# The first expert pair's weight chunks through both buffer rings, and less fill per expert step

## The chip, the cores and the metric

The kernel runs on one core of one Trainium2 chip, in one launch. The metric is the device time of that launch in microseconds (us); the median over several runs counts. TensorE is called PE below, VectorE DVE, ScalarE ACT, GpSimd POOL, SyncE SP.

## What is computed

Two transformer blocks follow each other on 512 tokens of width 1024, with a context of 256 tokens beside them. The first block mixes the tokens with three attention branches and then runs an expert-choice feed-forward layer: 16 experts, each of which takes the 64 tokens that its router column ranks highest.

```
def expert_choice_ffn(h, w_router, w_gate, w_up, w_down):
    ...
    gate, idx = lax.top_k(jnp.swapaxes(aff, 1, 2), cap)
    ...
    xe = h[bidx, idx]
    hid = jax.nn.silu(jnp.einsum('becd,edf->becf', xe, w_gate)) * jnp.einsum('becd,edf->becf', xe, w_up)
    ye = jnp.einsum('becf,efd->becd', hid, w_down) * gate[..., None].astype(h.dtype)
    return jnp.zeros_like(h).at[bidx, idx].add(ye)
```

The second block has two layers, each over the tokens and over the context (latent attention, pooling, gated linear attention, a gated merge). All is float32.

## The kernel before, in words

The program is written as Python generators that yield a nominal cost after each piece of work. `weave(main, fill, ratio)` takes a piece of `main` and then pieces of `fill` worth `ratio` times its cost, so two stages share the engines. A scheduler then orders each engine's instructions; every engine and every DMA queue works in that order.

The stage in question is the feed-forward layer of the first block. `ffn_start` norms the tokens, runs the router and the top-k. `experts` works on the 16 experts in 8 pairs, `p` = 0 to 7. A pair is 12 calls of `group`: 4 for the gate product, 4 for the up product, 4 for the down product. A group loads four chunks of expert weights (`we`, 128x1024 float32, 512 KB each, the DMA issues of L1296 on SP) and runs eight matmuls on them (L1307). So there are 96 groups and 384 chunks. Two experts share the PE array, 64 rows each.

Chunks land in one of two rings of buffers. `early` (tag "early", `NEARLY` = 20 buffers) lives only while the pool `tpR` is open. `big` (tag "wbig", `nbig` = 8 buffers) lives until the experts end. `s.pre` starts at `NPRE` = 44. In `body` (L2163 to L2180) the pool `tpR` is open while `ffn_start` and then the first 11 groups (44 chunks) are written out; after that the space of `tpR` is given to `tpB`, where the fill's tiles lie. A chunk may only be loaded into a buffer when the matmuls that read the buffer's last chunk are done, and SP issues in order: while one chunk waits for its buffer, all loads behind it wait.

From the twelfth group on the experts are woven with the fill, `ctx2(0)`, at `RATIO_E`. `ctx2(0)` is the first layer of the second block for the context: some seventy projections. A projection loads 512 KB of weights (`wr`, L412), ACT and DVE split them into a high and a low part (`wh` L395, `wl` L391), and PE runs 24 matmuls on them (L404 to L406, 128x256). Its last piece, `finish`, has 8 projections with `w_out` (`wr<-in_wout` on SP, stationary `wh`/`wl`, moving `mh`), a norm and a store.

After the experts, `ffn_end` adds their outputs to the tokens: for each of 8 column blocks a transpose of the summed outputs (L1417), a placing of the last pair's outputs (L1419), two DVE additions (L1421) and a square for the norm (L515, L516). It is woven with what is left of the fill at `RATIO_G` = 2, and its first yield is worth 10. Then the tokens' second block begins with the matmuls on `hx`.

Of the kernel before, what the change touches and what calls it, by code (L numbers as in the profile page):

```python
# [307 lines left out]
def weave(main, fill, ratio):  # L308

    while True:  # L310
        try:
            c = next(main)
        except StopIteration as e:
            return e.value
        fill.step(c * ratio)


class Kern:
# [967 lines left out]
    def experts(s):  # L1286
# [1 line left out]
        wx = s.d["wexp"]  # L1288

        def chunk(p, i, h):  # L1290
            if s.pre:
                s.pre -= 1
                w = s.early.tile([128, 1024], F32, name=s.uid("we"), tag="early", bufs=NEARLY)
            else:
                w = s.big.tile([128, 1024], F32, name=s.uid("we"), tag="wbig", bufs=s.nbig)
            nc.sync.dma_start(w, wx[p, i][:, h * 1024:h * 1024 + 1024])  # L1296
            return w

        def group(p, c0, stat, ps, kh):

            ws = [[chunk(p, c0 + e, h) for e in (1, 0)][::-1] for h in (1, 0)][::-1]
            with s.tc.high_priority(URGE):
                for h in range(2):
                    for kk in range(2):
                        k = 4 * kh + 2 * h + kk
                        for e in range(2):
                            nc.tensor.matmul(ps[64 * e:64 * e + 64, :], stat[:, k, 64 * e:64 * e + 64],  # L1307
                                             ws[h][e][:, kk * 512:kk * 512 + 512], start=k == 0, stop=k == 7)
# [801 lines left out]
def tags(w=512, **k):  # L2110
    return {a: b if isinstance(b, (tuple, str)) else (b, w) for a, b in k.items()}
# [3 lines left out]
NEARLY = 20  # L2115
URGE = 600
NPRE = 44
# [21 lines left out]
TAGS_M = tags(kc=(4, 256), P=(4, 768), PT=4)  # L2139
TAGS_F = tags(fx=8, ft=3)  # L2140
RATIO_G = 2
RATIO_E = 0.8
TAGS_G = tags(gh=8, gl=4)


def body(tc, d, out):
    from contextlib import ExitStack
    with ExitStack() as ctx:
# [26 lines left out]
        with k.pool("tpB") as tp:  # L2175
            k.where = (tp, TAGS_C)
            k.wq = tc.nc.sync
            fill.add(k.ctx2(0, M[0], cd, C[0]))
            weave(ex, fill, RATIO_E)
            big.close()  # L2180
# [36 lines left out]
```

## Time and profile before

| what | value |
|---|---|
| median of 3 runs | 2788.2 us (2779.96 to 2794.11) |
| the profiled execution | 2794.44 us, span of its instructions 2792.6 us |
| PE busy | 2625.3 us (94% of the span) |
| DVE, ACT busy | 1569.8 us, 1230.6 us |
| HBM traffic over the span | 191 GB/s on average |
| first and last start of an expert matmul (L1307) | 833.9 us, 1535.8 us |

The profile gives busy times of each engine over the span and in slices, groups of instructions with their idle time and its releaser, waits, and busy times with DMA rates in chosen stretches. Times within the execution count from the span's start.

### The profile page before, as it was taken

The numbers are of one execution on the slowest core, as the hardware profiler recorded it, in microseconds if no ns is written. First come the engines' busy times: TensorE is split into PE (matmuls) and PEld (weight loads), VectorE is DVE, ScalarE is ACT, GpSimd is POOL, SyncE is SP. The second block draws the span as 40 slices with busy tenths as digits, with TensorE's granted clock in tenths as the row PEclk, the third lists the DMA queues.
The fourth block names the chain that finished last, engine by engine and source line by source line (L and its number), as shares of the span: only waits on it lengthen the run. The fifth ranks groups of instructions, "written<-read, shape, count | busy, mean of one in ns | idle before, by whom it ended". The sixth has DMA issues, their size and how long they took to land. (4 is left out here: it accounts for less than half of the span.)

```text
span 2792.6 us, 41759 instructions
## 1 busy us (share of the span) xinstructions
PE 2625.3 (94%) x16372; PEld 1859.9 (67%) x16372; DVE 1569.8 (56%) x2957; ACT 1230.6 (44%) x2159; POOL 161.0 (6%) x260
## 2 busy tenths in 40 slices
PE   6999999999958999999998899999999999999997
PEld 2666677887633566555654577777777777777776
DVE  3564677676441324456232656656866546766974
ACT  3333355444222224365222444545655645555652
POOL 1000001110001000000000000000010000000001
PEclk9899999999979999999999899999999999999998
DMA  8545424634879999988999332213354332114353
GB/s 287 177 164 191 146 85 161 209 120 156 298 283 325 340 380 356 335 297 300 352 366 372 126 106 83 77 51 136 118 186 135 128 123 84 62 39 140 117 177 114
DMA packets 167974, 537.68 MB, mean 193 GB/s; under 512 B 21272, under 2 KB 22376, under 8 KB 167776
## 3 DMA queue, kind: packets, MB, share of 16 engines
q1 hardware_dynamic: 138528, 460.40, 47.2%
q0 software_dynamic: 17152, 52.57, 5.8%
q10 hardware_dynamic: 12096, 22.03, 2.1%
q8 instruction: 129, 2.11, 0.3%
q14 instruction: 69, 0.57, 0.1%
HBM read 484.06 MB, written 48.76 MB: 191 GB/s over the span
## 5 line engine op out<-in xcount | busy, mean ns | idle before, releaser
L391 DVE TENSOR_TENSOR wl<-wr,wh 128x1024 fp32r<-128x1024 f32 x320 | 390.8, 1223 | 386.8 <-ACT wh L395 357.3
L395 ACT CAST wh<-wr 128x1024 fp32r<-128x1024 f32 x320 | 334.4, 1047 | 458.2 <-PE ps L405 348.6
L404 PE MATMUL ps<-hx,wh 128*128 128x512 f32 x1168 | 473.8, 406 | 5.8 <-ACT hx L569 5.1
L405 PE MATMUL ps<-hx,wh 128*128 128x512 f32 x1168 | 468.8, 402 | 0.1
L406 PE MATMUL ps<-hx,wl 128*128 128x512 f32 x1168 | 466.9, 400 | 0.0
L404 PEld LDWEIGHTS ps<-hx,wh 128*128 128x128 f32 x1168 | 221.8, 190 | 66.9 <-issue 13.2
L1307 PE MATMUL ps<-we,xe 128*64 128x512 f32 x1024 | 241.1, 615 | 18.1 <-DMA we<-in_wexp 18.0
L405 PEld LDWEIGHTS ps<-hx,wh 128*128 128x128 f32 x1168 | 221.6, 190 | 52.3 <-issue 8.4
L406 PEld LDWEIGHTS ps<-hx,wl 128*128 128x128 f32 x1168 | 221.7, 190 | 50.2 <-issue 3.3
L673 ACT ACTIVATE P<-ps,st 128x768 f32<-128x768 f32 (+3 forms) x144 | 111.1, 771 | 142.6 <-DVE st L669 107.7
L1307 PEld LDWEIGHTS ps<-we,xe 128*64 128x64 f32 x1024 | 76.0, 141 | 144.8 <-issue 118.4
L404 PE MATMUL ps<-hc,wh 128*128 128x256 f32 x496 | 144.1, 291 | 0.1
L406 PE MATMUL ps<-hc,wl 128*128 128x256 f32 x496 | 139.8, 282 | 0.5 <-DVE wl L391 0.5
L405 PE MATMUL ps<-hc,wh 128*128 128x256 f32 x496 | 140.3, 283 | 0.0
L667 DVE TENSOR_REDUCE st<-ps 128x1 f32<-128x768 f32 (+3 forms) x144 | 114.2, 793 | 38.1 <-PE ps L406 35.3
L1307 PE MATMUL ps<-we,hT 128*64 128x512 f32 x512 | 122.8, 626 | 10.4 <-DMA we<-in_wexp 8.2
L695 PE MATMUL ps<-c_ident,P 128*128 128x128 f32 x688 | 110.0, 278 | 5.3 <-ACT PT L698 3.5
L404 PEld LDWEIGHTS ps<-hc,wh 128*128 128x128 f32 x496 | 94.1, 190 | 19.5 <-issue 14.2
L695 PEld LDWEIGHTS ps<-c_ident,P 128*128 128x128 f32 x688 | 79.9, 140 | 39.8 <-ACT PT L698 13.4
L471 PE MATMUL ps<-wm,sc_cc 128*32 128x512 f32 x384 | 89.4, 647 | 15.9 <-DMA wm<-in_wmod 14.1
L698 ACT COPY PT<-ps 128x512 f32<-128x512 f32 x123 | 70.1, 586 | 72.6 <-PE ps L695 71.9
L405 PEld LDWEIGHTS ps<-hc,wh 128*128 128x128 f32 x496 | 94.0, 190 | 4.0 <-issue 3.5
(517 smaller groups left out, 5036.1 us busy)
## 6 DMA issues: line engine op xcount, KB each, us to landing
we<-in_wexp SPq DMA_DIRECT2D x384, 512.0 KB
wr<-in_win SPq DMA_DIRECT2D x240, 512.0 KB
wm<-in_wmod SPq DMA_DIRECT2D x48, 512.0 KB
wr<-in_wbr SPq DMA_DIRECT2D x48, 512.0 KB
dram<-th ACTq DMA_DIRECT2D x72, 256.0 KB
mth<-dram SPq DMA_DIRECT2D x72, 256.0 KB
wr<-in_wout SPq DMA_DIRECT2D x32, 512.0 KB
dram<-mth POOLq DMA_DIRECT2D x48, 256.0 KB, 3.1
```

What stands on the lines that cost most here:

```text
L391: s.nc.vector.tensor_tensor(out, a, b, ALU.subtract)
L395: i = s.nc.scalar.copy(hi, src)
L404: t.matmul(out, a[0], b[0], start=start, stop=False)
L405: t.matmul(out, a[0], b[1], start=False, stop=False)
L406: t.matmul(out, a[1], b[0], start=False, stop=stop)
L471: nc.tensor.matmul(ps[32 * j:32 * j + 32, :], sc[:, k, :], w[:, j % 2 * 512:j % 2 * 512 + 512], start=k == 0, stop=k == 7)
L667: nc.vector.tensor_reduce(st[:, 0:1], sc[:, :n], AX.X, ALU.max)
L673: nc.scalar.activation(p[:, :n], sc[:, :n], AF.Exp, bias=st[:, 1:2], scale=scale, accum_out=st[:, 2:3])
L695: nc.tensor.transpose(tp[:, j:j + 128], blocks[(i + j) // 128], s.const("ident"))
L698: nc.scalar.copy(parts[i // 512][:, :m], tp[:, :m])
L1307: nc.tensor.matmul(ps[64 * e:64 * e + 64, :], stat[:, k, 64 * e:64 * e + 64], ws[h][e][:, kk * 512:kk * 512 + 512], start=k == 0, stop=k == 7)
```

## The change

Two things change. The choice of the ring now counts chunks modulo 28 (`NEARLY + s.nbig`): chunk numbers 0 to 7 go to `big`, 8 to 27 to `early`, 28 to 35 to `big` again, 36 to 42 to `early`, and number 43 and all later ones to `big`. Before, 0 to 43 went to `early` and all later ones to `big`. And `RATIO_E` goes from 0.8 to 0.7.

```diff
         def chunk(p, i, h):
-            if s.pre:
-                s.pre -= 1
+            n = (NPRE - s.pre) % (NEARLY + s.nbig)
+            s.pre = max(s.pre - 1, 0)
+            if s.pre and n >= s.nbig:
                 w = s.early.tile([128, 1024], F32, name=s.uid("we"), tag="early", bufs=NEARLY)
             else:
                 w = s.big.tile([128, 1024], F32, name=s.uid("we"), tag="wbig", bufs=s.nbig)
...
-RATIO_E = 0.8
+RATIO_E = 0.7
```

What this moves on SP, at the end of the first prefetch: the rows name the chunk's tile (`we` and its number in the order of the program: 1291 is the first, 1313 the twenty-first, 1346 to 1349 are the twelfth group, 1362 and 1363 belong to the second pair) and the semaphores that the issue waits for (`PE` among them: the buffer must have been read by its matmuls; `DMAHW`: an earlier transfer must have landed). Before:

```order
L1296 DMA we1311_6985<-in_wexp 128x1024 [waits DMAHW5_49]
L1296 DMA we1312_6987<-in_wexp 128x1024 [waits DMAHW6_49]
L1296 DMA we1346_7130<-in_wexp 128x1024 [waits DMAHW7_49]
L1296 DMA we1347_7132<-in_wexp 128x1024 [waits DMAHW0_49]
L1296 DMA we1348_7134<-in_wexp 128x1024 [waits DMAHW1_49]
L1296 DMA we1349_7136<-in_wexp 128x1024 [waits DMAHW2_49]
L1296 DMA we1362_7173<-in_wexp 128x1024 [waits DMAHW3_49]
L1296 DMA we1363_7175<-in_wexp 128x1024 [waits DMAHW4_49]
L1296 DMA we1313_6997<-in_wexp 128x1024 [waits DMAHW5_49,PE_49]
L1296 DMA we1314_6999<-in_wexp 128x1024 [waits DMAHW6_49,PE_49]
```

Now, from the same place on SP:

```order
L1297 DMA we1312_6987<-in_wexp 128x1024 [waits DMAHW6_49,DVE_49]
L1297 DMA we1313_6997<-in_wexp 128x1024 [waits DMAHW7_49]
L1297 DMA we1314_6999<-in_wexp 128x1024 [waits DMAHW0_49,PE_49]
L1297 DMA we1315_7001<-in_wexp 128x1024 [waits DMAHW1_49]
L1297 DMA we1316_7003<-in_wexp 128x1024 [waits DMAHW2_49]
L1297 DMA we1318_7014<-in_wexp 128x1024 [waits DMAHW3_49]
L1297 DMA we1319_7016<-in_wexp 128x1024 [waits DMAHW4_49]
L1297 DMA we1320_7018<-in_wexp 128x1024 [waits DMAHW5_49]
L1297 DMA we1321_7020<-in_wexp 128x1024 [waits DMAHW6_49]
L1297 DMA we1322_7030<-in_wexp 128x1024 [waits DMAHW7_49,PE_49]
```

Before, the twenty chunks of the small ring were followed by six chunks of later groups, and only then by the twenty-first chunk. Now 28 chunks follow each other in the order in which PE reads them; we1322 is the twenty-ninth, the first that waits for an expert matmul.

On PE, around the last expert group (we and hT are the operands of an expert matmul, oh and ye those of the placing, fo that of the transposes, hc and mh those of the fill). Before:

```order
L1307 MATMUL ps_12837<-we_12871,hT_12258 64x512
L1307 MATMUL ps_12837<-we_12869,hT_12258 64x512
L1417 MATMUL ps_12962<-c_ident,fo_12775 128x128
L1417 MATMUL ps_12962<-c_ident,fo_12777 128x128
L1417 MATMUL ps_12962<-c_ident,fo_12779 128x128
L1417 MATMUL ps_12962<-c_ident,fo_12781 128x128
L516 MATMUL ps_12938<-sq_12959,sqw 2x512
L1419 MATMUL ps_12963<-oh_12773,ye_12783 128x512
```

Now the last expert matmul is followed by a projection on `hc` (24 matmuls, of which the first three stand here), and at once after it by the 192 matmuls on `mh` of the 8 projections with `w_out`:

```order
L1308 MATMUL ps_12459<-we_12491,hT_11898 64x512
L1308 MATMUL ps_12459<-we_12489,hT_11898 64x512
L404 MATMUL ps_12511<-hc_7291,wh_12507 128x256
L405 MATMUL ps_12511<-hc_7292,wh_12507 128x256
L406 MATMUL ps_12511<-hc_7291,wl_12508 128x256
```

and those end, before the placing begins, with

```order
L404 MATMUL ps_12852<-mh_12591,wh_12848 128x256
L405 MATMUL ps_12852<-mh_12592,wh_12848 128x256
L406 MATMUL ps_12852<-mh_12591,wl_12849 128x256
L1420 MATMUL ps_12889<-oh_12317,ye_12327 128x512
L1420 MATMUL ps_12889<-oh_12317,yl_12457 128x512
L1420 MATMUL ps_12910<-oh_12317,ye_12327 128x512
```

So 216 matmuls, nine projections, that stood among the experts' groups now stand between the experts and `ffn_end`. From the end of `ffn_end` on, the order of every engine is the same as before.

## Rows read from the trace of the kernel before

**Rows 1.** The page, parts 1 and 2: busy times, and 40 slices of the span.

```profile
PE 2625.3 (94%) x16372; PEld 1859.9 (67%) x16372; DVE 1569.8 (56%) x2957; ACT 1230.6 (44%) x2159; POOL 161.0 (6%) x260
...
PE   6999999999958999999998899999999999999997
...
DMA  8545424634879999988999332213354332114353
```

**Rows 2.** Stretches: us, PE, PEld, DVE, ACT, POOL busy (instructions), PE clock, DMA share, GB/s.

```profile
834.00:919.20 85.20, 68.77 (x295) 25.33 (x295) 14.60 (x34) 14.75 (x29) 12.69 (x16) 0.91 0.87 312
919.20:1536.40 617.20, 584.76 (x3974) 352.70 (x3972) 247.06 (x532) 226.87 (x443) 34.02 (x37) 0.98 0.95 345
1536.40:1564.60 28.20, 18.81 (x65) 7.33 (x65) 17.79 (x28) 11.03 (x18) 0.00 (x0) 0.83 0.34 121
```

**Rows 3.** SP's timeline in three windows: start, length, issue, count.

```profile
785.34 36.39 SPq L1296 DMA_DIRECT2D we<-in_wexp  x26
...
836.39 29.19 SPq L1296 DMA_DIRECT2D we<-in_wexp  x26
...
883.13 5.99 SPq L1296 DMA_DIRECT2D we<-in_wexp  x8
```

**Rows 4.** Stretches of the first pair, columns as in the stretches above.

```profile
836.00:840.00 4.00, 4.00 (x20) 1.31 (x18) 0.00 (x0) 0.00 (x0) 0.00 (x0) 1.00 0.60 184
844.00:872.00 28.00, 27.38 (x134) 11.66 (x130) 3.33 (x5) 2.25 (x4) 3.72 (x6) 1.00 1.02 396
876.00:880.00 4.00, 3.89 (x12) 1.21 (x14) 0.00 (x0) 0.00 (x0) 0.00 (x0) 0.57 0.11 42
880.00:884.00 4.00, 4.00 (x22) 1.34 (x20) 0.70 (x2) 0.00 (x0) 1.59 (x3) 1.00 0.22 59
```

**Rows 5.** PE's timeline, first pair: start, length, work, count, idle before and its releaser.

```profile
833.86 28.31 PE L1307 MATMUL ps<-we,xe 128*64 128x512 f32 x128
...
864.89 7.09 PE L1307 MATMUL ps<-we,hT 128*64 128x512 f32 x32 [0.24 <-ACT hT L1348]
876.11 8.71 PE L1307 MATMUL ps<-we,hT 128*64 128x512 f32 x32 [4.14 <-DMA we<-in_wexp]
...
895.82 5.66 PE L1307 MATMUL ps<-we,xe 128*64 128x512 f32 x16 [4.94 <-DMA we<-in_wexp]
```

**Rows 6.** PE's timeline later: two expert groups, between them one projection.

```profile
922.29 3.65 PE L1307 MATMUL ps<-we,xe 128*64 128x512 f32 x16
925.87 0.38 PE L404 MATMUL ps<-hc,wh 128*128 128x256 f32 x1
...
928.77 3.65 PE L1307 MATMUL ps<-we,xe 128*64 128x512 f32 x16
```

**Rows 7.** Four stretches, 919.2 to 1536.4 us, columns as above.

```profile
919.20:1200.00 280.80, 273.98 (x1664) 166.65 (x1662) 106.05 (x219) 97.49 (x183) 16.60 (x17) 1.00 0.97 354
1200.00:1330.00 130.00, 117.28 (x1162) 71.41 (x1159) 79.60 (x219) 77.41 (x179) 5.20 (x4) 0.95 0.86 297
1330.00:1455.00 125.00, 122.10 (x761) 76.18 (x758) 37.82 (x54) 32.44 (x49) 5.73 (x4) 1.00 0.97 356
1455.00:1536.40 81.40, 71.41 (x394) 38.45 (x394) 23.60 (x41) 19.52 (x34) 6.50 (x12) 0.96 1.01 373
```

**Rows 8.** PE's waits: us in total, times, longest; 919.2 to 1536.4 us.

```profile
PE ps L1307 <- DMA we<-in_wexp: 12.0, 11, 3.5
...
PE ps L404 <- ACT mth L628: 1.4, 3, 0.5
```

**Rows 9.** PE's waits, 1455 to 1536.4 us.

```profile
PE ps L1307 <- DMA we<-in_wexp: 8.3, 5, 3.5
```

**Rows 10.** PE's timeline after the last expert matmul.

```profile
1540.02 0.66 PE L1417 MATMUL ps<-c_ident,fo 128*128 128x128 f32 x4 [3.64 <-DVE x L1421]
...
1564.58 1.65 PE L404 MATMUL ps<-hx,wh 128*128 128x512 f32 x3 [1.36 <-ACT hx L569]
```

**Rows 11.** DVE's groups of the fill's end, 1500 to 1537 us: count, busy us, mean ns, idle.

```profile
L2002 DVE SCALAR_TENSOR_TENSOR o<-o,G,rb 128x256 f32<-128x256 f32 x8 | 3.5, 480 | 5.4 <-ACT rb L557 5.4
L2003 DVE TENSOR_TENSOR o<-o,xr 128x256 f32<-128x256 f32 x8 | 3.0, 418 | 0.0
```

## The prediction

> **What bounds the kernel now.** The page comes first. PE is busy for 94% of the span, and its digits are 9 nearly everywhere; the DMA digits are 8 or 9 only in a block that is the expert stage [rows 1]. There two resources are close to full together, so the question is what each lacks in that stage. I cut it into three by the stretches view [rows 2]. From 834.0 us (first expert matmul) to 919.2 us there is no fill; PE has 68.8 of 85.2 us, and the DMA engines are 0.87 busy. From 919.2 us to the last expert matmul at 1536.4 us the fill stands among the groups: PE 584.8 of 617.2 us, so 32.4 us idle, and 345 GB/s, which is 213 MB. From there to the first matmul on hx at 1564.6 us `ffn_end` runs alone: 28.2 us, PE 18.8 us.
>
> In the first stretch the cause of the idle time can be read from SP. It issued 26 chunks by 821.7 us and then nothing until 836.4 us; again 26 until 865.6 us, and nothing until 883.1 us [rows 3]. The second hole shows in the DMA rates: 396 GB/s from 844 to 872 us, then 42 and 59 GB/s from 876 to 884 us [rows 4]. SP stood at the 53rd chunk, whose buffer in the ring of 8 held the first chunk of the twelfth group. That group could not be read earlier, since the eleventh waited 4.14 us for its own chunks and then ran 8.71 us for two groups where 7.09 us is usual [rows 5]; the clock in that stretch was 0.57 [rows 4].
>
> In the second stretch PE waited only 12.0 us for expert chunks [rows 8], and 8.3 us of it in the last 81 us [rows 9].
>
> **The ring.** By the order, 28 chunks come before the first expert wait, in the order in which PE reads them. At 396 GB/s a chunk (0.524 MB) takes 1.32 us [rows 4]. The first 26 were issued by 821.7 us, so two more fit in the 14.7 us of SP's hole and are there when PE starts. From then on chunk 28 and the following wait for the same matmuls as the 27th issue did. SP gets to the eleventh group's chunks eight places earlier in its order, so they have landed before 872.0 us, when PE finishes the tenth group (864.89 + 7.09). The 4.14 us wait goes, and so do the 1.62 us that groups eleven and twelve lost at the lower clock: **-5.8 us**. This is carried on only if SP's next stop moves too. It does: after number 50, chunk 51 now waits for number 43, which the eleventh group reads, and chunk 52 for number 44, the twelfth group's first. Both groups come 5.8 us earlier, so the transfers resume about then, and PE's next wait, the 4.94 us at 895.8 us [rows 5], stands 5.8 us earlier. It does not vanish: from the second pair on there are still 8 buffers. Bounds: 0, if other transfers fill the time, and -10.7, if the 4.94 us went as well.
>
> **The fill, until the last expert matmul.** Nine projections move behind it. A projection among the groups costs PE 2.9 us (925.87 to 928.77) [rows 6], but behind one another 24 matmuls of 0.117 us follow closer; I take 2.8 us, so 25.2 us of PE work leave the stretch. They take 4.7 MB of loads along, which leaves 208.3 MB. If the idle time stayed as it is, the stretch would take 592 us. But lighter fill between groups calls for chunks at a higher rate. The stretch from 1200 to 1330 us (gated linear attention: small steps, PE 117.3 of 130 us, 297 GB/s, 38.6 MB) [rows 7] has room and stays as it is. The rest, 487.2 us before, moved 174.4 MB at 358 GB/s; now it has 169.7 MB for 462 us, 367 GB/s. The waits for chunks by rate: 3.7 us in 405.8 us (0.9%) where 354 to 356 GB/s flowed, 8.3 us in 81.4 us (10%) at 373 [rows 7 to 9]. On a line between them, 361 GB/s is where the waits (4%, 18 us instead of 12) and the rate agree: 469 us. So the stretch takes 599 us by that line. I take 597 us, a little below, since the row at 373 GB/s holds three groups that had no fill at all: **-20 us**. Bounds: -37 us if no wait for chunks is left (25.2 + 12.0), and -10 us if 355 GB/s is all that these mixed transfers reach (169.7 MB in 478 us, and 130).
>
> One page speaks against the change here. The Trainium skill (DMA: Bandwidth & Descriptors, section Bandwidth) says that for transfers from HBM to SBUF the HBM side binds, at about 358 GB/s for a core, though it lists 425 GB/s measured with one core. By the 358 this stretch would be at its limit already, the term -13 us, and the sum +7 us. The 396 GB/s above [rows 4] don't agree with it.
>
> **Behind the last expert matmul.** The 25.2 us of projections come back, at full price: nothing else is on PE then, and the transfers are idle enough to feed them (0.34 busy before [rows 2]). The projections on mh need the last merge's result through ACT and DVE; waits of that kind were at most 0.5 us [rows 8], while PE's longest on DVE here was 3.64 us [rows 10]: I take **+2 us**. `ffn_end` loses those 3.64 us, since the last experts' outputs are long ready when it starts. But the norm and the additions of the fill's end (16 DVE instructions, 6.5 us [rows 11]), until now beside the experts, stand beside its 16 additions; DVE was busy 17.8 of 28.2 us [rows 2], so most fits in its gaps: +2 us, between 0 and 6.5. Together **+25.6 us**, between 22.1 and 31.7.
>
> **Sum.** -5.8 - 20 + 25.6 = -0.2 us on the profiled execution's 2794.4 us. That one is 6.2 us above the median of the runs, 2788.2 us, so I predict **2788 us**. A measurement of this kernel can tell about 0.5%, 14 us, from no change. The order after `ffn_end` is the same, and the work before 785 us too, so nothing else should move.
>
> **Rivals.** *The transfers follow* (0.20). If they give what the first pair shows, 396 GB/s, the waits for chunks go and the fill covers the experts to the end: -5.8 - 37 + 22 to 25 = -18 to -21 us, 2767 to 2770 us; half of that gain and a ring term near -10.7 reach 2774 too. For it: 8.3 of the 12.0 us fell where the fill had run out. Against: 373 GB/s with a DMA share of 1.01 there. *The transfers are the limit* (0.13), which ends slower: at 355 GB/s the experts shorten by 10 us only, while 25.2 us of PE work now run after them with the DMA engines half empty: -5.8 - 10 + 25.6 to 31.7 = +10 to +16 us, 2798 to 2804 us. It decides once the stretch shortens by less than 20 us. For it: DMA shares of 0.97 in the long stretches [rows 7]. *The ring does nothing* (0.17): 26 chunks were there before, 28 now, and the 4.14 us come back as a longer wait when the second pair begins, since its first chunks no longer lie ready. Then the sum is +5.6 us, 2794 us.
>
> **How the numbers follow.** The forecast itself (0.50) reaches 9 us to both sides for the bounds of its terms, 2779 to 2797 us. Ends of 2770 and 2803 us leave out the far part of both outer rivals, some 0.2 in all. Below 2774 us lies most of the first rival and a little of the forecast: faster 0.20. Above 2802 us lie the far half of the second rival and a bad tail term: slower 0.12. The rest, 0.68, is no change that can be told.
>
> **What would show it.** Ring: SP's first run of issues has 28 chunks, the 4.14 us wait before the eleventh group is gone, and the 42 to 59 GB/s hole lies earlier; the matmuls of the second pair then begin some 6 us sooner. Fill: no stretch without projections before the last expert matmul, that matmul at about 1510 us (833.9 + 79.4 + 597), PE's waits for chunks 12 to 20 us in total. End: hx begins at about 1564 us. If hx begins before 1550 us or after 1578 us, the prediction is wrong; the stretch with the fill, at 580 or at 607 us, would tell which rival it was.

## The result, and the profile after

The changed kernel takes 2805.11 us (median of 9 runs, 2795.02 to 2815.78) against 2788.2 us before (2779.96 to 2798.21): a ratio of 1.0056, 95% interval 1.0035 to 1.0077. It is slower, by a little more than the half per cent that a measurement can tell, and 2 us above the upper end of the range. The profiled execution took 2806.96 us, with a span of 2805.2 us.

The line numbers behind the ring's changed lines are one higher than before: chunks are issued at L1297, expert matmuls are L1308. Lengths below are counted from the first expert matmul, since its own start lies between 826.7 and 833.9 us in the profiled executions of all kernels, also of the one with the old ring (826.7), whose work before it is the same as in the kernel before.

| part of the profiled execution | before | after | difference | forecast |
|---|---|---|---|---|
| first expert matmul to the end of the 17th group | 85.4 us | 82.0 us | -3.4 | -5.8 |
| from there to the last expert matmul | 617.1 us | 599.0 us | -18.2 | -20 |
| from there to the first matmul on `hx` | 28.2 us | 66.0 us | +37.8 | +25.6 |
| sum | 730.7 us | 747.0 us | +16.2 | -0.2 |
| from `hx` to the end | 1228.0 us | 1227.8 us | -0.2 | 0 |

The page's first parts look like [rows 1]: 8 us more of PE, and digits that hardly differ.

```profile
PE 2633.7 (94%) x16372; PEld 1866.4 (67%) x16372; DVE 1569.0 (56%) x2957; ACT 1232.5 (44%) x2159; POOL 160.1 (6%) x260
...
PE   6999999999958999999998899999999999999997
```

The same three parts as stretches (columns as in [rows 2]):

```profile
830.40:912.40 82.00, 70.00 (x296) 27.00 (x295) 14.59 (x34) 14.56 (x29) 11.25 (x16) 0.91 0.94 331
912.40:1511.30 598.90, 560.95 (x3743) 328.65 (x3743) 225.63 (x491) 210.92 (x408) 32.36 (x33) 0.97 0.95 344
1511.30:1577.40 66.10, 51.10 (x297) 37.53 (x295) 38.13 (x69) 29.01 (x53) 2.15 (x4) 0.89 0.43 148
```

PE's busy time in the middle row fell by 23.8 us, the work of the nine projections, but its idle time rose from 32.4 to 38.0 us. In the last row 32.3 us of PE work came back, beside 15.0 us of idle time instead of 9.4 us. (This row's edges are rounded outward; the table counts from the matmuls themselves.) The two idle times and the price of the work behind the experts are what has to be explained.

**The ring.** SP's timeline of the changed kernel, in three windows (start, length, issue, count; answers to [rows 3]):

```profile
782.85 40.76 SPq L1297 DMA_DIRECT2D we<-in_wexp  x28
...
833.24 13.75 SPq L1297 DMA_DIRECT2D we<-in_wexp  x15
...
857.27 19.24 SPq L1297 DMA_DIRECT2D we<-in_wexp  x13
```

28 chunks are issued ahead, then 15, and SP stops at 847.0 us with 43 chunks out: number 43 is next. PE's timeline of the changed kernel in the first pair and the second (answers to [rows 5]):

```profile
830.41 28.60 PE L1308 MATMUL ps<-we,xe 128*64 128x512 f32 x128
...
861.73 14.00 PE L1308 MATMUL ps<-we,hT 128*64 128x512 f32 x64 [0.24 <-ACT hT L1349]
878.63 5.35 PE L1308 MATMUL ps<-we,xe 128*64 128x512 f32 x16 [2.90 <-DMA we<-in_wexp]
...
887.84 6.51 PE L1308 MATMUL ps<-we,xe 128*64 128x512 f32 x16 [2.28 <-DMA we<-in_wexp]
896.60 8.78 PE L1308 MATMUL ps<-we,xe 128*64 128x512 f32 x32 [2.25 <-DMA we<-in_wexp]
908.72 3.65 PE L1308 MATMUL ps<-we,xe 128*64 128x512 f32 x16 [3.33 <-DMA we<-in_wexp]
```

The wait of 4.14 us before the eleventh group is gone; the last four groups of the first pair are one row of 64 matmuls in 14.00 us. Up to the end of the twelfth group the changed kernel is 5.6 us ahead (45.3 us against 51.0). Then four waits for chunks, 10.8 us together, stand before groups 13, 14, 15 and 17, and at the end of the 17th group 3.4 us are left.

The kernel before has four waits there as well, of nearly the same length. PE's waits from the end of the 12th group to the end of the 17th (us in total, times, longest), and the same stretches (columns as in [rows 2]), first before, then changed:

```profile
PE ps L1307 <- DMA we<-in_wexp: 10.1, 4, 4.9
PE ps L1308 <- DMA we<-in_wexp: 10.8, 4, 3.3
...
884.80:919.30 34.50, 22.81 (x89) 7.19 (x84) 10.12 (x26) 9.63 (x19) 7.37 (x7) 0.85 0.98 328
875.70:912.40 36.70, 25.30 (x88) 8.35 (x87) 10.12 (x26) 9.52 (x19) 5.49 (x7) 0.81 0.95 325
```

The five groups and the few matmuls beside them take 25.3 us of PE instead of 22.8, at a granted clock of 0.81 instead of 0.85. That is the larger part of the 2.2 us that are lost again; the waits for chunks add 0.7 us, and the short waits on the fill's norm take 1.0 us off.

**The middle.** PE's waits from 912.4 to 1511.3 us (us in total, times, longest; answers to [rows 8]):

```profile
PE ps L1308 <- DMA we<-in_wexp: 11.3, 12, 2.4
PE ps L1418 <- DMA fo<-dram: 3.7, 1, 3.7
```

The waits for chunks do not grow. A wait of 3.7 us for `fo`, the experts' outputs read back for `ffn_end`, now falls ahead of the last expert matmul.

The same stretch in three parts: to the first matmul of the fill's gated linear attention, that attention to its last matmul, and the rest (columns as in [rows 2]). First the outer two before, whose middle one stands at e7 below, then all three of the changed kernel:

```profile
919.20:1205.60 286.40, 278.66 (x1696) 170.43 (x1694) 108.66 (x222) 102.67 (x190) 17.02 (x18) 1.00 0.97 353
1310.50:1536.40 225.90, 212.10 (x1290) 129.94 (x1290) 70.42 (x111) 61.52 (x99) 13.23 (x17) 0.98 0.98 359
...
912.40:1214.70 302.30, 290.03 (x1714) 170.27 (x1714) 107.09 (x221) 99.77 (x184) 17.63 (x18) 0.99 0.98 356
1214.70:1337.30 122.60, 108.06 (x1068) 59.99 (x1067) 70.79 (x203) 70.74 (x165) 6.11 (x4) 0.93 0.86 299
1337.30:1511.30 174.00, 162.86 (x963) 98.39 (x963) 47.76 (x68) 40.41 (x59) 8.62 (x11) 0.97 0.96 355
```

Outside the gated linear attention the transfers run no faster than before: 356 and 355 GB/s, where they had 353 and 359. Beside it stand 15 expert groups now, where there were 13.

**Behind the last expert matmul.** SP's timeline of the changed kernel, 1480 to 1580 us:

```profile
1499.59 0.63 SPq L412 DMA_DIRECT2D wr<-in_wout  x1
1504.45 10.07 SPq L1406 DMA_DIRECT2D x<-dram  x8
1514.62 23.94 SPq L412 DMA_DIRECT2D wr<-in_wout  x7
```

Of SP's waits in the changed kernel from 1490 to 1560 us, the one that holds them (us in total, times, longest):

```profile
SPq L1406 <- PE ps L1308: 10.6, 2, 6.5
```

Eight loads of `x` (L1406, for `ffn_end`) stand on SP between the first `w_out` load and the other seven. They go to the pool "fe", which takes the place of `big`, and so wait for the last expert matmuls to have read their chunks: 10.6 us. The seven loads behind them, on which the projections on `mh` rest, start at 1514.62 us, after the last expert matmul, when PE already wants them. PE's timeline of the changed kernel shows the price in one row:

```profile
1522.11 0.58 PE L404 MATMUL ps<-mh,wh 128*128 128x256 f32 x1 [3.55 <-ACT wh L395]
```

Two stretches of the changed kernel, the one behind that wait, and `ffn_end` (columns as in [rows 2]):

```profile
1522.00:1528.50 6.50, 5.93 (x26) 5.64 (x27) 2.45 (x2) 1.14 (x3) 0.00 (x0) 0.50 0.46 160
...
1547.50:1577.40 29.90, 20.65 (x78) 8.65 (x76) 21.29 (x43) 11.68 (x21) 0.00 (x0) 0.87 0.26 89
```

After the 3.55 us wait the granted clock is 0.50 for 6.5 us, the lower level of 1.2 GHz: 26 instructions take 5.93 us. The nine projections end at 1547.2 us, 35.8 us after the last expert matmul. What is left, 30.2 us, is `ffn_end`; it was 28.2 us before, with 17.8 us of DVE (28 instructions), and has 21.3 us of DVE (43 instructions) now.

### The profile page after: what moved, and what is told of

Its sections match the earlier page's. It is cut to its first block, busy times and chain, and to the rows that moved or that the text cites. A ratio compares the mean times of both kernels' runs of the same rounds, so it can differ in the third digit from the quotient of the medians.

```text
span 2805.2 us, 41737 instructions
## 1 busy us (share of the span) xinstructions
PE 2633.7 (94%) x16372; PEld 1866.4 (67%) x16372; DVE 1569.0 (56%) x2957; ACT 1232.5 (44%) x2159; POOL 160.1 (6%) x260
## 5 line engine op out<-in xcount | busy, mean ns | idle before, releaser
L1308 PE MATMUL ps<-we,xe 128*64 128x512 f32 x1024 | 243.4, 622 | 21.4 <-DMA we<-in_wexp 21.3
L1308 PEld LDWEIGHTS ps<-we,xe 128*64 128x64 f32 x1024 | 75.2, 142 | 152.0 <-issue 127.5
L1308 PE MATMUL ps<-we,hT 128*64 128x512 f32 x512 | 118.5, 608 | 2.9 <-ACT hT L1349 1.9
L404 PEld LDWEIGHTS ps<-hc,wh 128*128 128x128 f32 x496 | 95.1, 192 | 28.1 <-issue 23.9
L404 PE MATMUL ps<-mh,wh 128*128 128x512 f32 (+1 forms) x256 | 95.9, 375 | 3.6 <-ACT wh L395 3.6
```

The source lines that it names most:

```text
L404: t.matmul(out, a[0], b[0], start=start, stop=False)
```

## The experiments

Ratios are to the kernel before on the same chip. The lengths are those of the table above, from each kernel's profiled execution. Several ratios (e1, e5, e6, e9) differ from 1 by less than the half per cent that the prediction held to be measurable, though their intervals leave out 1; e1 and e9 overlap each other.

| kernel | to the end of group 17 | to the last expert matmul | from there to `hx` | sum | ratio (95% interval) |
|---|---|---|---|---|---|
| before | 85.4 | 617.1 | 28.2 | 730.7 | 1 |
| changed | 82.0 | 599.0 | 66.0 | 747.0 | 1.0056 (1.0035 to 1.0077) |
| e1, ring alone | 84.0 | 617.8 | 28.2 | 730.0 | 0.9981 (0.9967 to 0.9995) |
| e2, ratio alone | 84.6 | 607.0 | 64.6 | 756.2 | 1.0076 (1.0050 to 1.0103) |
| e3, loads of `x` later | 84.3 | 596.0 | 61.2 | 741.5 | 1.0049 (1.0033 to 1.0064) |
| e4, fill spread in `ffn_end` | 81.6 | 595.3 | 61.6 | 738.5 | 1.0063 (1.0041 to 1.0085) |
| e5, e3 and e4 together | 81.9 | 598.9 | 59.0 | 739.9 | 1.0022 (1.0004 to 1.0040) |
| e6, fill not woven | 82.2 | 599.9 | 58.0 | 740.1 | 1.0026 (1.0008 to 1.0045) |
| e7, `RATIO_E` 0.77 | 82.3 | 638.3 | 33.2 | 753.8 | 1.0050 (1.0033 to 1.0067) |
| e8, `RATIO_E` 0.9 | 82.9 | 676.5 | 27.0 | 786.4 | 1.0172 (1.0145 to 1.0200) |
| e9, ring alone, 48 chunks | 88.7 | 607.1 | 28.2 | 724.1 | 0.9966 (0.9951 to 0.9980) |
| e10, ring alone, 56 chunks | 83.3 | 641.5 | 32.7 | 757.6 | 1.0070 (1.0045 to 1.0094) |

### e1 and e2: each half of the change alone

e1 is the changed kernel with the old ratio, e2 the kernel before with the new one.

```diff
e1: -RATIO_E = 0.7
    +RATIO_E = 0.8
e2: -RATIO_E = 0.8
    +RATIO_E = 0.7
```

> The new choice of rings with RATIO_E back at 0.8. Theory A (the ring gains a little, the lighter fill loses more): first expert matmul to the end of group 17 takes 82 us as in the changed kernel (85.2 before), everything behind it is as before (617 us to the last expert matmul, 28 us from there to hx), so 3 us less than the kernel before in all, ratio 0.999. Rival B (the ring itself costs, because from chunk 43 on only 8 buffers are left while SP already stands): the stretch to the last expert matmul grows by 5 us or more, ratio 1.002 or above.

> The kernel before with RATIO_E 0.7 and nothing else. Theory A: 85 us to the end of group 17, about 599 us from there to the last expert matmul (18 less than before), 66 us from there to hx (38 more), so about 20 us more than before in all, ratio 1.007. Rival B: the ring is what costs, so this one stays within 5 us of the kernel before, ratio below 1.002.

e1 takes 2782.8 us and is a little faster than the kernel before, e2 is slower. The product of the two ratios, 0.9981 x 1.0076 = 1.0057, is the ratio of the change, 1.0056: within their intervals the two halves add up, and all of the loss is the ratio's. The profiled executions do not add up so well: -0.7 and +25.5 us against +16.2. Most of that is the stretch to the last expert matmul, 607.0 us in e2, with 17.6 us of waits for chunks, and 595.3 to 599.9 us in the five kernels that have the same ratio and the new ring. So the ring may help there too, which one execution of e2 can't show. In e1's profile 4.5 us are gained up to the end of the twelfth group (46.5 us against 51.0) and 1.4 us are left at the end of the 17th; the other parts keep their lengths within 1 us. Its sum explains 0.7 us of the 5 us that the runs show; the rest can't be placed with one execution of each.

### e3: the loads of `x` behind the projections' loads

```diff
         x, f = [], s.f
+        yield 10.0
         for k in range(8):
             t = s.T(nm="x", tag="fx")
             nc.sync.dma_start(t, xd[k])
             x.append(t)
-        yield 10.0
```

> The changed kernel, with the 8 loads of x for the end of the layer written behind its first yield, so that they no longer stand ahead of the w_out loads on SP. Theory A (SP's queue starves the projections: seven of the eight w_out loads stand behind loads that wait for the last expert matmul): the nine projections after the last expert matmul take 27 to 29 us instead of 35.8, the 3.55 us wait on the split weights and the half clock after it go, 7 us less than the changed kernel in all. Rival C (two raw buffers and the split on ACT and DVE set the pace, whatever the order): still 34 us or more.

SP's timeline of e3, 1480 to 1580 us:

```profile
1496.08 0.56 SPq L412 DMA_DIRECT2D wr<-in_wout  x1
1501.03 0.33 SPq L1407 DMA_DIRECT2D x<-dram  x1
1506.06 1.59 SPq L412 DMA_DIRECT2D wr<-in_wout  x2
```

The two stretches of e3 behind the last expert matmul, the nine projections and then `ffn_end` (columns as in [rows 2]):

```profile
1507.90:1537.10 29.20, 27.02 (x218) 25.86 (x218) 16.49 (x26) 16.66 (x32) 2.15 (x4) 1.00 0.73 240
1537.10:1569.10 32.00, 21.43 (x78) 9.31 (x76) 21.48 (x43) 12.12 (x21) 0.00 (x0) 0.80 0.24 83
```

One `x` load instead of eight stands ahead of the next `w_out` loads, the wait for `wh` is gone, the granted clock is 1.00 throughout, and the nine projections take 29.1 us instead of 35.8. So 6.7 us of the overrun were the queue. e2, which has the same order on SP as the changed kernel, bears it out: 34.6 us for the nine projections. `ffn_end` gives 2 us of it back (32.0 us), and the ratio moves only from 1.0056 to 1.0049, within both intervals, so these times do not settle it. The times of e5 and e4 below, which differ by this edit alone, support it: 1.0022 and 1.0063, each against the kernel before on its own chip, with intervals that do not overlap. They differ by some 11 us, though, where the two profiled executions differ by 2.6 us behind the experts.

### e4, e5, e6: another order behind the experts

```diff
e4: -RATIO_G = 2
    +RATIO_G = 1
e5: e3 and e4 together
e6: -RATIO_G = 2
    +RATIO_G = 0
```

> The changed kernel with RATIO_G 1 instead of 2: half of the w_out projections stand ahead of the end of the layer, the rest among its eight steps. Theory A (the end of the layer leaves PE idle for want of work, which the projections could fill): from the last expert matmul to hx 52 to 56 us instead of 66, 10 to 14 us less than the changed kernel. Rival D (DVE is what paces those steps): 63 us or more.

> The changed kernel with both earlier edits: the loads of x behind the first yield of the layer's end, and RATIO_G 1. Theory A (two separate losses behind the last expert matmul: w_out loads stuck on SP, and too little for PE among the layer's last steps): 54 to 58 us from the last expert matmul to hx, against 66 in the changed kernel and 61 to 62 with either edit alone; ratio to the kernel before 1.002 to 1.004. Rival E (one loss, that both edits mend): 60 us or more, ratio 1.005 or above.

> The changed kernel with RATIO_G 0: nothing of the fill is written ahead of the layer's end, the eight w_out projections follow it and cover its last steps and the norm behind it. Theory A (what costs is where the left-over projections stand, ahead of a chain of small steps that PE then has to itself): from the last expert matmul to hx 48 to 54 us, ratio 1.000 to 1.003. Rival D (DVE paces it, wherever they stand): 60 us or more, ratio 1.005 or above.

With a lower `RATIO_G` the projections are spread among `ffn_end`'s pieces, so that DVE's additions and PE's projections can lie beside each other. From the last expert matmul to `hx` it takes 61.6, 59.0 and 58.0 us instead of 66.0. All three are longer than expected (52 to 56, 54 to 58 and 48 to 54 us) and shorter than their rivals said (63, 60 and 60 us or more). It helps and is not enough: even the best of them adds 29.8 us there (58.0 - 28.2), where the stretch before gained 17.2 us. e4 shows no gain in its ratio; e5 and e6 come back to 1.0022 and 1.0026, still slower than before. So no order of this work behind the experts that was tried pays for what it saves among them.

### e7 and e8: more fill per group, not less

The changed kernel (with its ring) and another ratio: 0.77, at which the fill ends with the last group, and 0.9, at which it ends well before.

```diff
e7: -RATIO_E = 0.7
    +RATIO_E = 0.77
e8: -RATIO_E = 0.7
    +RATIO_E = 0.9
```

> The changed kernel with RATIO_E 0.77, at which the order has the fill's last projection just ahead of the last expert group and none behind it. Theory A (only the projections left behind the experts cost; until then the lighter fill gains its own work and no more): 610 to 615 us from group 17 to the last expert matmul, 28 to 31 us to hx, ratio 0.996 to 0.999, as the ring alone or 3 us better. Rival F (any fill below 0.8 leaves PE waiting for chunks through the whole stage): PE waits for chunks 15 us or more in that stretch and the ratio is 1.000 or above.

> The changed kernel with RATIO_E 0.9, at which the fill ends some ten groups ahead of the last expert matmul. Theory A: the groups without fill wait for their chunks, about 2 us each; waits for chunks 20 to 30 us in the stretch from group 17 to the last expert matmul, which takes 623 to 630 us; then 28 us to hx; ratio 0.999 to 1.003. Rival G (transfers have room and a denser fill costs nothing): 617 us and ratio 0.998, as at 0.8.

Both are misses. e7 was expected at 610 to 615 us up to the last expert matmul and took 638.3; e8 was expected at 623 to 630 and took 676.5. Where it went is seen in the stretch of the gated linear attention, from its first matmul to its last (columns as in [rows 2]). In the kernel before:

```profile
1205.60:1310.50 104.90, 93.99 (x989) 52.34 (x990) 67.99 (x200) 62.68 (x155) 3.78 (x3) 0.93 0.85 291
```

The same part in e7:

```profile
1218.00:1328.60 110.60, 91.88 (x957) 51.12 (x956) 67.11 (x189) 67.80 (x158) 3.92 (x3) 0.87 0.81 276
```

The same part in e8, and behind it the stretch to the last expert matmul:

```profile
1200.50:1306.10 105.60, 81.85 (x896) 49.20 (x896) 64.88 (x186) 65.67 (x157) 1.06 (x2) 0.81 0.54 188
1306.10:1592.10 286.00, 245.94 (x1404) 139.93 (x1403) 74.02 (x115) 65.36 (x104) 17.41 (x19) 0.95 0.94 337
```

This part of the fill is a chain of small steps between PE, ACT and DVE, and it takes 105 to 111 us in all three. What differs is how many expert groups stand beside it: 13 before, 11 in e7, 8 in e8. With fewer groups PE is idle for 10.9, 18.7 and 23.8 us, its granted clock falls from 0.93 to 0.87 and 0.81, and the transfers run at 188 GB/s in e8, between stretches at 338 and 337. The groups that are left over come later, where the transfers have no slack: in e8's last row PE waits 30.7 us for chunks. So too few groups there cost time in e7 and e8. That the count is the cause is argued and not shown, and it is not all: e9 below has 12 groups and does it in 96.8 us, and the changed kernel has 15 groups, is idle for 14.5 us of its 122.6, and has a granted clock of 0.93. The count went unlooked at when the ratio's effect was worked out. For e7 this explains 14 us of the 20 us that the stretch to the last expert matmul took over 617.8 (7.2 us longer with two groups fewer, 3.5 us for a group); the rest stays open.

### e9 and e10: more chunks in the wide ring

e1 with 48 and with 56 chunks in the two rings instead of 44. The fill then begins after the 12th and the 14th group instead of the 11th.

```diff
e9:  -NPRE = 44
     +NPRE = 48
e10: -NPRE = 44
     +NPRE = 56
```

> The ring edit with the fill's ratio of before (0.8), and 48 chunks of the ring instead of 44, so that chunks 43 to 46 stand in the wide ring of 20 and it is chunk 47 that waits for chunk 28. Theory (the ring gives back in the second pair because chunk 43 already waits for the eighth group): the hole in SP's issues comes four chunks later and is shorter, the waits before groups 13 to 17 (10.8 us in all in the changed kernel) shrink by 3 to 5 us, and the end of the 17th group stands 79 to 81 us after the first expert matmul (84.0 with the ring alone, 82.0 in the changed kernel); ratio to before 0.996 to 0.999. Rival (the second pair waits for its gather and its turn, or the transfers are at their limit there): 82 to 84 us as with the ring alone, ratio 0.998. Second rival: the fill begins a group later, and what is gained is lost beside the gated linear attention: until the last expert matmul over 620 us, ratio over 1.0.

> The same with 56 chunks, two whole rounds of 28, so that chunk 55 is the first to wait for chunk 28. Theory: SP's issues go on without a hole until then, and the transfers of the first 17 groups run at the 396 GB/s of the first pair: the end of the 17th group stands 72 to 78 us after the first expert matmul; ratio 0.993 to 0.998 if the rest keeps its length (617.8 us until the last expert matmul). Rival (the second pair's gather and turn, or the limit of the transfers): 82 to 84 us, ratio 0.998 or above. Second rival: the fill begins three groups later, so its first steps have fewer groups beside them: the end of the 17th group comes early, but the stretch from there to the last expert matmul grows by as much or more (over 623 us), ratio 0.998 to 1.005.

e9 has the lowest ratio of the study: 2781.89 us against 2790.38 us before on that chip. SP's timeline of e9 in two windows:

```profile
834.00 32.98 SPq L1297 DMA_DIRECT2D we<-in_wexp  x27
...
874.75 35.60 SPq L1297 DMA_DIRECT2D we<-in_wexp  x17
```

PE's timeline of e9 around the start of the second pair:

```profile
876.27 7.09 PE L1308 MATMUL ps<-we,xe 128*64 128x512 f32 x32
897.12 0.98 PE L497 MATMUL ps<-ones,sq 128*128 128x1 f32 x4 [13.76 <-DVE sq L545]
...
899.50 9.83 PE L1308 MATMUL ps<-we,xe 128*64 128x512 f32 x32
912.89 6.53 PE L1308 MATMUL ps<-we,xe 128*64 128x512 f32 x16 [3.55 <-DMA we<-in_wexp]
```

The ring does what the theory says: SP issues 27 chunks on end instead of 15, to 867.0 us, and groups 13 and 14 start without a wait for chunks, where the changed kernel waits 5.2 us before them. (Groups 15 and 16 don't wait either, but only after a long stop of PE, in which their chunks had time to land.) But the end of the 17th group does not come earlier, it comes at 88.7 us, later than in any other kernel. PE stands 13.76 us in front of the fill's first step, the sum of squares for the context's norm (L497). ACT's waits in e9, 860 to 900 us, say for what (us in total, times, longest):

```profile
ACT sq L542 <- DMA c<-in_cT: 16.2, 6, 8.8
```

The context tiles `c` lie in the space of `tpR`, which is now held until the 12th group has been read, and their loads come late. POOL's timeline of e9 shows where they stand:

```profile
861.46 1.19 POOL L384 DMA_DIRECT2D c<-in_cT  x2
877.50 1.53 POOL L1383 DMA_INDIRECT dram<-ye,idx  x1 [14.85 <-ACT ye L1377]
878.47 2.80 POOL L384 DMA_DIRECT2D c<-in_cT  x4
886.02 1.52 POOL L1383 DMA_INDIRECT dram<-ye,idx  x1 [4.75 <-DMA dram<-ye,idx]
887.41 0.76 POOL L384 DMA_DIRECT2D c<-in_cT  x1
```

Six of the eight loads stand behind the store of the first pair's outputs (L1383), which waits 14.85 us for ACT, and two of them behind the second such store, which waits 4.75 us for the first. In the changed kernel all eight are issued by 869.8 us, ahead of both. It is the trap of the `x` loads again, on POOL's queue; how much of the delay is this order and how much the space is not shown. All later groups stand behind that step in PE's order. The expectation (79 to 81 us) was wrong on this, and the gain comes from the next part instead: 607.1 us to the last expert matmul, with 5.9 us of waits for chunks instead of 11.6 in e1, and a granted clock of 0.98 beside the gated linear attention instead of 0.95. Why is not shown; some of it may only have crossed the boundary, since the 17th group ends 4.7 us later than in e1. A version that keeps the wide ring and starts the fill's norm later was not tried.

e10 misses its theory (72 to 78 us) and comes nearest to its second rival, but its 17th group does not end early and its ratio lies above that rival's: 83.3 us, and then 641.5 us. PE stands 13.35 us before L497 here too. The fill begins after the 14th group, 11 groups are left beside the gated linear attention (271 GB/s, granted clock 0.89), and PE waits 18.5 us for chunks up to the last expert matmul.

## Why the prediction was wrong

**The fill until the last expert matmul (-20 us): right in size, not in its working.** It came to -18.2 us. The forecast added 6 us of waits for chunks, 18 us in all; they were 11.3 us. The other idle time was thought to stay and rose by 6 us, 3.7 of them the wait for `fo`. That the two are alike is luck. The forecast also had the transfers outside the gated linear attention rise, from 358 to 361 GB/s by its own, wider cut. They were 353 and 359 GB/s before and 356 and 355 after. That is the figure of the rival that the transfers are the limit, and the upper end of that rival's sum, +10 to +16 us, is what was measured. Against it stand the waits for chunks, which did not grow, and the -18.2 us, where it said -10. In e2, with the old ring, it would be nearly right: -10.1 us, with 17.6 us of waits. No run tells the two apart, so this rival stays open. By the rule of the Trainium skill (DMA: Bandwidth & Descriptors, section Bandwidth) the term was estimated at -13 us and the sum at +7 us. Its 358 GB/s is close to the rates of these stretches; as a bound it does not agree with the 396 GB/s over 28 us in [rows 4]. That section also ties it to two cores that stream at once, and here one core ran.

**Behind the last expert matmul (+25.6 us): this is the step that failed.** It came to +37.8 us. The step said that the projections come "at full price: nothing else is on PE then, and the transfers are idle enough to feed them". The DMA engines did have room, 0.43 busy over the whole stretch; the queue that issues to them was not free. The term counted PE's work and the bandwidth and not the order of SP, in which eight loads of `x` that wait for the last expert matmuls stand ahead of seven of the eight `w_out` loads. The nine projections were priced at 25.2 us, with 2 us of waits 27.2, and took 35.8: 8.6 us too little, of which e3 shows 6.7 to be this queue (a 3.55 us wait, and half clock behind it); the other 1.9 us stay open. The other 3.6 us are `ffn_end`: I took its 3.64 us wait on DVE away and charged 2 us for the fill's norm and additions. It took 30.2 us, not 26.6. DVE's busy time rose from 17.8 to 21.3 us there. Its length goes with whether the fill's last norm and additions fall into it in the other runs too, though no run changed that alone: with 28 DVE instructions it takes 28.2 us (before, e1, e9), with 43 it takes 30.2 us (changed), 32.0 (e3), 33.2 (e7) and 32.7 us (e10). The upper end for that piece, 6.5 us, was nearer than the 2 us that I took.

**The ring (-5.8 us): right about the wait, wrong about what follows it.** The 4.14 us wait and the low clock went as said, and 5.6 us were there at the end of the twelfth group. But the step went on: "after number 50, chunk 51 now waits for number 43", so that SP's next stop would come as much earlier and the lead be carried on. SP stopped at number 43 itself. That chunk and all later ones are sent to the 8 buffers of `big`, whose buffer 0 holds chunk 28, which the eighth group reads; so 13 of the 20 buffers of `early` stand idle from there on. The stop lasted from 847.0 to 857.3 us, the end of which is where the eighth group runs (830.41 and seven groups of 3.58 us make 855.4). The transfers show it mildly: 328 GB/s from 840 to 872 us, where e9, without this stop, has 363 GB/s from 834 to 867 us. The second pair then waits for chunks four times, as it did before (10.8 and 10.1 us), but now already ahead of group 13, and runs its groups at a lower clock: 2.5 us more of PE. Over the eight kernels with this ring and 44 chunks the end of the 17th group lies at 81.6 to 84.3 us, against 84.6 and 85.4 us with the old ring: a gain of 0.3 to 3.8 us. e9 supports the reading: with four more chunks in the rings the stop at 43 and the waits before groups 13 and 14 are gone. The rival that the ring does nothing is half true.

**The sum.** -3.4 - 18.2 + 37.8 makes +16.2 us where -0.2 was said. The ring and the middle fell short by 2.4 and 1.8 us; 12.2 of the 16.4 us are the step behind the experts. The test that was set, `hx` not after 1578 us, was passed at 1577.4, because this execution's first expert matmul came 3.5 us early, which shows that it should have been counted from there. The upper bound for that term, 31.7 us, was too low as well, since it held no wait for a load at all.

## What to carry to other kernels

Before work is moved to a place with idle engines and idle transfers, read the issuing queue's order at that place: a load that waits for a buffer holds every load behind it, however idle the DMA engines are. Here it was SP's queue behind the experts and, in e9, POOL's ahead of the fill. Work that fills another stage's gaps is worth more where it is than its busy time says, on both sides: here 18 us were gained by taking nine projections from among the experts, and 30 to 38 us paid to run them alone. When a ring gets more buffers, follow it to the chunk at which the wide ring ends; a lead that is won before that point can be given back behind it (here 5.6 us became 3.4), and moving that stop alone did not bring the 17th group's end forward (e9).

## What the runs showed of the hardware that was not expected

- The granted clock fell where PE idled in the gated linear attention: idle for 10.9 us of 105 it had 0.93 (before), for 18.7 us of 111 it had 0.87 (e7), for 23.8 us of 106 it had 0.81 (e8). In e7 PE has the same fill there as before (781 matmuls) and two groups less, some 7 us, but its busy time fell by 2.1 us only (93.99 to 91.88 us), so the gaps are paid for again in the work between them. It isn't strict: e9 idled 12.1 us of 97 there and had 0.98, the changed kernel 14.5 us of 123 and had 0.93.
- One wait of 3.55 us was followed by 6.5 us at 0.50, in which 26 instructions took 5.93 us.
